# Gated linear attention on 64x64 tiles of the TensorE array, in steps by head pairs

## The chip, the cores and the metric

The kernel runs on one NeuronCore of a Trainium2 chip. The metric is device time in microseconds (us) of one execution. Lower is better.

## The reference, cut to what matters

The kernel is one whole layer: normalization, one large projection, three attention branches, a gated merge, an output projection, and a squared-ReLU MLP, on 512 frames of 1024 channels. The change is in branch A, gated linear attention, with 4 heads, 64 key channels, 128 value channels and chunks of 64 frames:

```python
b = jnp.cumsum(log_a, axis=2)              # inside each chunk of 64
e_pos, e_neg = jnp.exp(b), jnp.exp(-b)
q_pos = qc * e_pos
a_causal = einsum('bnthd,bnshd->bnhts', q_pos, kc * e_neg)
a_anti   = einsum('bnthd,bnshd->bnhts', qc * e_neg, kc * e_pos)
attn = jnp.where(lower, a_causal, a_anti)
o_intra = einsum('bnhts,bnshv->bnthv', attn, vc)
chunk_kv = einsum('bnshd,bnshv->bnhdv', kc * jnp.exp(b_last - b), vc)
state    = state * chunk_decay + chunk_kv   # scan over 8 chunks; prev is the state before each
o_inter  = einsum('bnthd,bnhdv->bnthv', q_pos, prev)
o = o_intra + o_inter                       # then RMSNorm by head and a SiLU gate
```

Per head and chunk the products are small: scores contract over 64 channels, states over 64 frames, and the read of a state (the chunk product) over 64 channels.

## The kernel before

TensorE's order is the program's order; the other engines are scheduled by the framework. The large products split each operand into a high and a low part and run three matmuls (`mm3`, L151 to L153). Weights stream in as chunks of 128x1024: a DMA, a cast to the high part on ScalarE (L142), a subtraction for the low part on VectorE (L143).

The attention of branch A stands in the block `with pool("gla")`. Its work is a list of 20 steps, which `weave` mixes with 96 units of filling: the gate and output projection of the memory branch (`branch("gate_mem", ...)`). A unit is one `mm3`. After step i (counted from 0) the filling is brought up to 96 × (i + 1) // 20 units, so that about five units lie behind each step. An `idle` step is filling alone.

Heads go in pairs: pair j holds heads 2j and 2j + 1, whose 64 channels share the 128 partitions of the projected q and k (`gqT[j]`, `gkT[j]`). The steps are:

- `decays(j)`: sums of log decays on TensorE (L686), three exponentials, and the scaled keys `kn`, `kp`, `kd`. The scaled queries `qpos[e]`, `qneg[e]` exist once per head e of the pair (L707, L708): the other head's 64 partitions are zero, filled once by GpSimd (L677, L678).
- `key_turn(j)`: four transposes of `kd` (L715), copied to two tiles, `kdE` for even chunks (VectorE, L716) and `kdO` for odd chunks (ScalarE, L717). Each is zero in the other half of its partitions (L679, L680).
- `gla_scores(h)`: four matmuls for the causal and four for the mirrored scores (L748). Each takes all 128 partitions, of which the zeros in `qpos[e]` leave one head. The masks select from both into the tile `at`, in copies of 128x128 (L750).
- `states(j)`: sixteen matmuls over all 128 partitions, 64 columns each; the two heads' results go to the two partition halves (L729). VectorE then runs the scan into `prev` (L734, L736).
- `gla_values(h)`: per block of two chunks the scores times v, full width (L759; the first block in two halves, L763), alternating with the two chunk products `qpos` times `prev` of 64 columns each (L765). Square, sum, reciprocal root (GpSimd, L231) and scaling to `on` (L774) follow.
- `gla_turn(h)`: four transposes of `on` (L780), the gate (L782) and a split for the output projection.

PSUM tiles of these steps come from `at_()`, four banks in rotation.

Of the kernel before, what the change touches and what calls it, by code (L numbers as in the profile page):

```python
# [9 lines left out]
F32 = mybir.dt.float32  # L10
# [3 lines left out]
AF = mybir.ActivationFunctionType  # L14
ALU = mybir.AluOpType
AX = mybir.AxisListType

P = 128
D = 1024
S = 512  # L20
M = 256
KT = D // P
NT = S // P
# [38 lines left out]
def hybrid_block(ctx, tc, chunks, wst, xT, memT, xN, cols, gffn, gfin, wup, cst, out):  # L62
    nc = tc.nc
# [5 lines left out]
    def nm(s):  # L69
        uid[0] += 1  # L70
        return f"{s}_{uid[0]}"
# [13 lines left out]
    def at_(shape=None):  # L85
        return pa.tile(shape or [P, 512], F32, tag="a", name=nm("a"))
# [140 lines left out]
    def rsqrt(pool_, ss, inv, n):  # L227
        ms = pool_.tile([P, n], F32, tag="ms", name=nm("ms"), bufs=2)
        r = pool_.tile([P, n], F32, tag="rr", name=nm("rr"), bufs=2)
        nc.vector.tensor_scalar(ms, ss, inv, EPS, op0=ALU.mult, op1=ALU.add)  # L230
        nc.gpsimd.tensor_tensor(r, ms, mhalf[:, :n], op=ALU.pow)  # L231
        return r
# [34 lines left out]
    with pool("front") as fp:  # L267
# [24 lines left out]
        ps = at_()  # L292
# [375 lines left out]

    with pool("gla") as lp:
        NC = 8  # L670
        qpos = [lp.tile([P, S], F32, name=f"qpos{e}") for e in range(2)]
        qneg = [lp.tile([P, S], F32, name=f"qneg{e}") for e in range(2)]
        kdE = lp.tile([P, NT, P], F32, name="kdE")
        kdO = lp.tile([P, NT, P], F32, name="kdO")
        for e in range(2):
            b = slice(64 - 64 * e, 128 - 64 * e)
            nc.gpsimd.memset(qpos[e][b], 0.0)  # L677
            nc.gpsimd.memset(qneg[e][b], 0.0)  # L678
        nc.gpsimd.memset(kdE[64:128], 0.0)  # L679
        nc.gpsimd.memset(kdO[0:64], 0.0)  # L680
        gs = {}

        def decays(j):
            pb = at_()
            for t in range(NT):
                nc.tensor.matmul(pb[:, t * P:(t + 1) * P], la[:, t, j * P:(j + 1) * P], tri64, start=True, stop=True)  # L686
            ep = lp.tile([P, S], F32, tag="ep", name=nm("ep"))
            en = lp.tile([P, S], F32, tag="en", name=nm("en"))
            bl = small(lp, NC, "bl").rearrange("p (c o) -> p c o", o=1)
            dec = small(lp, NC, "dec")  # L690
            ek = lp.tile([P, NC, 64], F32, tag="ek", name=nm("ek"))
            pb3 = pb.rearrange("p (c t) -> p c t", c=NC)
            nc.vector.tensor_copy(bl, pb3[:, :, 63:64])
            nc.vector.tensor_tensor(ek, pb3, bl.to_broadcast([P, NC, 64]), op=ALU.subtract)
            nc.scalar.activation(ep, pb, AF.Exp)
            nc.scalar.activation(en, pb, AF.Exp, scale=-1.0)
            nc.scalar.activation(ek, ek, AF.Exp, scale=-1.0)
            nc.scalar.activation(dec, bl.rearrange("p c o -> p (c o)"), AF.Exp)
            kn = lp.tile([P, S], F32, tag="kn", name=nm("kn"))
            kp = lp.tile([P, S], F32, tag="kp", name=nm("kp"))  # L700
            kd = lp.tile([P, S], F32, tag="kd", name=nm("kd"))
            nc.vector.tensor_tensor(kd, gkT[j], ek.rearrange("p c t -> p (c t)"), op=ALU.mult)
            nc.vector.tensor_tensor(kn, gkT[j], en, op=ALU.mult)
            nc.vector.tensor_tensor(kp, gkT[j], ep, op=ALU.mult)
            for e in range(2):
                a = slice(64 * e, 64 * e + 64)
                nc.vector.tensor_tensor(qpos[e][a], gqT[j][a], ep[a], op=ALU.mult)  # L707
                nc.vector.tensor_tensor(qneg[e][a], gqT[j][a], en[a], op=ALU.mult)  # L708
            gs["d", j] = dec, kn, kp, kd

        def key_turn(j):
            kd = gs["d", j][3]
            pk = at_([P, NT, P])
            for t in range(NT):
                nc.tensor.transpose(pk[:, t, :], kd[:, t * P:(t + 1) * P], ident)  # L715
            nc.vector.tensor_copy(kdE[0:64], pk[0:64])  # L716
            nc.scalar.copy(kdO[64:128], pk[64:128])  # L717

        def states(j):
            dec = gs["d", j][0]  # L720
            prev = gs["s", j] = lp.tile([P, NC, P], F32, tag="prev", name=nm("prev"))
            for g in range(2):
                pv = at_([P, 4, P])
                for i in range(4):
                    c = 4 * g + i
                    t = c // 2
                    for e in range(2):
                        h = 2 * j + e
                        nc.tensor.matmul(pv[64 * e:64 * e + 64, i, :], (kdO if c % 2 else kdE)[:, t, 64 * e:64 * e + 64],  # L729
                                         gv[:, t, h * P:(h + 1) * P], start=True, stop=True)  # L730
                for i in range(4):
                    c = 4 * g + i
                    if c == 0:
                        nc.vector.tensor_copy(prev[:, 1, :], pv[:, 0, :])  # L734
                    elif c < NC - 1:
                        nc.vector.scalar_tensor_tensor(prev[:, c + 1, :], prev[:, c, :], dec[:, c:c + 1], pv[:, i, :],  # L736
                                                       op0=ALU.mult, op1=ALU.add)

        def gla_scores(h):
            j, e = divmod(h, 2)  # L740
            _, kn, kp, _ = gs["d", j]
            pc, pn = at_([P, NT, P]), at_([P, NT, P])
            at = gs["a", h] = lp.tile([P, NT, P], F32, tag="at", name=nm("at"), bufs=2)
            nc.gpsimd.memset(at, 0.0)
            for m, (ps, kk, qq) in enumerate(((pc, kn, qpos[e]), (pn, kp, qneg[e]))):
                for t in range(NT):
                    sl = slice(t * P, (t + 1) * P)
                    nc.tensor.matmul(ps[:, t, :], kk[:, sl], qq[:, sl], start=True, stop=True)  # L748
                for t in range(NT):
                    nc.vector.copy_predicated(at[:, t, :], msk_s[:, m, :], ps[:, t, :])  # L750

        def gla_values(h):
            j, e = divmod(h, 2)
            at, prev = gs["a", h], gs["s", j]
            po = at_([P, NT, P])
            for t in range(NT):
                vt = gv[:, t, h * P:(h + 1) * P]
                if t:
                    nc.tensor.matmul(po[:, t, :], at[:, t, :], vt, start=True, stop=False)  # L759
                for c in (2 * t, 2 * t + 1):  # L760
                    r = slice(64 * (c % 2), 64 * (c % 2) + 64)
                    if t == 0:
                        nc.tensor.matmul(po[r, t, :], at[:, t, r], vt, start=True, stop=c == 0)  # L763
                    if c:
                        nc.tensor.matmul(po[r, t, :], qpos[e][:, 64 * c:64 * c + 64], prev[:, c, :], start=False,  # L765
                                         stop=True)
            sq = lp.tile([P, NT, P], F32, tag="sq", name=nm("sq"))
            ss = lp.tile([P, NT], F32, tag="ss", name=nm("ss"), bufs=2)
            nc.scalar.activation(sq, po, AF.Square)
            nc.vector.tensor_reduce(ss, sq, axis=AX.X, op=ALU.add)  # L770
            r = rsqrt(lp, ss, 1.0 / P, NT)
            on = gs["o", h] = lp.tile([P, NT, P], F32, tag="on", name=nm("on"), bufs=2)
            for t in range(NT):
                nc.vector.tensor_scalar(on[:, t, :], po[:, t, :], r[:, t:t + 1], None, op0=ALU.mult)  # L774

        def gla_turn(h):
            on = gs["o", h]
            pt = at_()
            for t in range(NT):
                nc.tensor.transpose(pt[:, t * P:(t + 1) * P], on[:, t, :], ident)  # L780
            og = lp.tile([P, S], F32, tag="og", name=nm("og"))
            nc.vector.tensor_tensor(og, pt, sg[h], op=ALU.mult)  # L782
            split(ogh[h], ogl[h], og)

        def idle(_):
            pass

        steps = [partial(fn, i) for fn, i in (
            (decays, 0), (idle, 0), (idle, 0), (key_turn, 0), (gla_scores, 0), (states, 0), (gla_scores, 1), (gla_values, 0), (gla_values, 1),
            (decays, 1), (gla_turn, 0), (gla_turn, 1), (key_turn, 1), (gla_scores, 2), (states, 1), (gla_scores, 3),  # L790
            (gla_values, 2), (gla_values, 3), (gla_turn, 2), (gla_turn, 3))]
        weave(steps, 96, branch("gate_mem", "w_mem_o", omh, oml, 1))
    gst.close()
    omst.close()
# [452 lines left out]
```

## Time and profile before

| | |
|---|---|
| median of 3 runs | 866.18 us (865.49 to 867.07) |
| span of the profiled execution, first to last instruction | 862.5 us |
| what lies around the span (median less span) | 3.7 us |
| TensorE clock granted, mean | 0.990 |
| the 20 steps with their filling | about 318 to 409 us of the span |

The time of the profiled execution itself is known by its span alone; the median is from executions without the profiler. In the profile, PE is the matmuls of TensorE and PEld its weight loads, which overlap; DVE is VectorE, ACT ScalarE, POOL GpSimd, SP the queue that issues most DMAs. `L729` is line 729 of the kernel. `out<-in` names the tiles, `x32` counts instructions. `a` stands for the PSUM tiles of `at_()`, `mm` for those of the large products. In the chain of waits a row is the start, the length, and the piece of work on the path that ended last.

### The profile page before, as it was taken

How to read it: one execution, taken by the hardware profiler on the slowest of the kernel's cores; microseconds unless marked ns; L12 is line 12 of the kernel's file. 1: busy time of each engine (PE TensorE's matmuls, PEld its weight loads, DVE VectorE, ACT ScalarE, POOL GpSimd, SP SyncE). 2: the span in 40 equal slices, each digit the busy share in tenths (PEclk: the TensorE clock that was granted, in tenths of full speed). 3: DMA queues.
4: the chain of work that ended last, by engine and by line, in shares of the span. 5: the costliest groups of instructions: out<-in, count | busy, mean ns of one | idle time of the engine just before them, and what ended most of it. 6: DMA issues, size and time to landing. Idle time of an engine off the chain costs nothing.

```text
span 862.5 us, 11811 instructions
## 1 busy us (share of the span) xinstructions
PE 839.0 (97%) x4513; PEld 711.2 (82%) x4513; DVE 542.4 (63%) x850; ACT 440.3 (51%) x703; POOL 113.0 (13%) x130
## 2 busy tenths in 40 slices
PE   8999999999999999999999999999999999999993
PEld 6778788888888888787888889888997899799872
DVE  5784656756444546474533547675688678778954
ACT  7764746754333432321332436565676377457744
POOL 5100000000000021221112100111001000100234
PEclk9999999999999999999999999999999999999997
DMA  8444745544547355336222413758757956785694
GB/s 320 145 150 168 201 135 178 146 171 123 171 133 230 125 150 168 97 113 231 98 98 98 170 50 118 225 124 204 243 171 162 265 199 171 179 256 176 138 170 133
DMA packets 37513, 142.37 MB, mean 165 GB/s; under 512 B 4592, under 2 KB 5392, under 8 KB 35728
## 3 DMA queue, kind: packets, MB, share of 16 engines
q1 hardware_dynamic: 27216, 93.36, 30.5%
q0 software_dynamic: 8448, 45.09, 24.8%
q10 hardware_dynamic: 1792, 3.16, 1.1%
q8 instruction: 35, 0.57, 0.3%
q14 instruction: 22, 0.18, 0.1%
HBM read 136.34 MB, written 27.28 MB: 190 GB/s over the span
## 4 chain that ended last, share of the span: by engine, by line
PE 74%; issue 12%; DMA 6%; DVE 3%; ACT 2%; POOL 1%; SPq 0%; POOLq 0%; ACTq 0%; DVEq 0%
PE mm L152 20%; PE mm L153 20%; PE mm L151 20%; DMA b<-in_wst_dram 6%; PE a L151 2%; PE a L152 2%; PE a L153 2%; ACT hi L203 1%; PE a L748 1%; DVE lo L204 1%; PE a L477 1%; DMA cst_s<-in_cst_dram 1%; PE a L765 1%; PE a L508 1%; PE a L507 1%
## 5 line engine op out<-in xcount | busy, mean ns | idle before, releaser
L143 DVE TENSOR_TENSOR wlo<-raw,whi 128x1024 fp32r<-128x1024 f32 x80 | 101.7, 1275 | 104.1 <-ACT whi L142 103.5
L142 ACT CAST whi<-raw 128x1024 fp32r<-128x1024 f32 x80 | 84.1, 1053 | 132.3 <-PE mm L152 100.3
L151 PE MATMUL mm<-uhi,whi 128*128 128x512 f32 x360 | 142.5, 396 | 0.0
L152 PE MATMUL mm<-ulo,whi 128*128 128x512 f32 x360 | 140.7, 391 | 1.4 <-DVE ulo L204 1.4
L153 PE MATMUL mm<-uhi,wlo 128*128 128x512 f32 x360 | 140.5, 390 | 0.0
L203 ACT CAST hi<-raw 128x1024 fp32r<-128x1024 f32 x58 | 60.5, 1048 | 44.7 <-PE mm L152 31.7
L204 DVE TENSOR_TENSOR lo<-raw,hi 128x1024 fp32r<-128x1024 f32 x58 | 70.6, 1222 | 17.6 <-ACT hi L203 17.6
L152 PEld LDWEIGHTS mm<-ulo,whi 128*128 128x128 f32 x360 | 67.7, 188 | 15.8 <-DVE ulo L204 2.9
L153 PEld LDWEIGHTS mm<-uhi,wlo 128*128 128x128 f32 x360 | 67.6, 188 | 14.6 <-DVE wlo L143 0.4
L151 PEld LDWEIGHTS mm<-uhi,whi 128*128 128x128 f32 x360 | 67.7, 188 | 13.5 <-issue 0.7
L204 DVE TENSOR_TENSOR lo<-b,hi 128x1024 fp32r<-128x1024 f32 x40 | 48.9, 1223 | 38.3 <-ACT hi L203 38.2
L203 ACT CAST hi<-b 128x1024 fp32r<-128x1024 f32 x40 | 41.9, 1048 | 57.5 <-PE mm L153 24.1
L152 PE MATMUL mm<-lo,ch 128*128 128x512 f32 x160 | 63.4, 396 | 2.5 <-DVE lo L204 2.5
L151 PE MATMUL mm<-hi,ch 128*128 128x512 f32 x160 | 63.1, 395 | 0.9 <-ACT hi L203 0.8
L153 PE MATMUL mm<-hi,cl 128*128 128x512 f32 x160 | 63.0, 394 | 0.0
L1050 POOL DMA_DIRECT2D b<-in_wst_dram x32 | 27.7, 865 | 267.1 <-DVE lo L204 210.2
L152 PE MATMUL mm<-u2l,hi 128*128 128x256 f32 x192 | 54.3, 283 | 0.0
L153 PE MATMUL mm<-u2h,lo 128*128 128x256 f32 x192 | 54.3, 283 | 0.0
L151 PE MATMUL mm<-u2h,hi 128*128 128x256 f32 x192 | 54.3, 283 | 0.0
L151 PE MATMUL mm<-u2sh,hi 128*128 128x256 f32 x144 | 40.8, 283 | 0.0
L152 PE MATMUL mm<-u2sl,hi 128*128 128x256 f32 x144 | 40.8, 283 | 0.0
L153 PE MATMUL mm<-u2sh,lo 128*128 128x256 f32 x144 | 40.8, 283 | 0.0
(349 smaller groups left out, 1945.5 us busy)
## 6 DMA issues: line engine op xcount, KB each, us to landing
raw<-in_wst_dram SPq DMA_DIRECT2D x122, 512.0 KB, 4.0
b<-in_wst_dram POOLq DMA_DIRECT2D x32, 512.0 KB, 5.3
T<-in_wst_dram POOLq DMA_DIRECT2D x12, 1024.0 KB, 8.4
raw<-T SPq DMA_DIRECT2D x24, 512.0 KB, 4.5
b<-in_wst_dram SPq DMA_DIRECT2D x16, 512.0 KB, 5.1
xr<-in_xT_dram SPq DMA_DIRECT2D x4, 512.0 KB, 8.1
nFb<-dF ACTq DMA_DIRECT2D x8, 256.0 KB, 3.8
h<-in_xN_dram SPq DMA_DIRECT2D x4, 512.0 KB, 7.6
```

Source lines behind the costliest of these rows:

```text
L142: cast = nc.scalar.copy(hi, raw)
L143: nc.vector.tensor_tensor(lo, raw, f(hi), op=ALU.subtract)
L151: nc.tensor.matmul(ps, lh, rh, start=start, stop=False)
L152: nc.tensor.matmul(ps, lh, rl, start=False, stop=False)
L153: nc.tensor.matmul(ps, ll, rh, start=False, stop=stop)
L203: nc.scalar.copy(hi, src)
L204: return nc.vector.tensor_tensor(lo, src, f(hi), op=ALU.subtract).ins
L477: nc.tensor.matmul(ps[:, :w], q, K[e][:, 1, :w], start=False, stop=True)
L507: nc.tensor.matmul(po[:, q0:], vv, PTh[:, c0:c0 + w], start=n == 0, stop=False)
L508: nc.tensor.matmul(po[:, q0:], vv, PTl[:, c0:c0 + w], start=False, stop=n == 3)
L748: nc.tensor.matmul(ps[:, t, :], kk[:, sl], qq[:, sl], start=True, stop=True)
L1050: nc.gpsimd.dma_start(to, x, accum_op=ALU.add)
```

## The change

The zero padding goes. `qpos` and `qneg` are one tile for a pair, `kdT` replaces `kdE` and `kdO`, and the memsets for zeros are gone. Every small matmul names its 64 partitions (`half[e]`): scores contract over 64 rows, and the two heads of a pair stand next to each other in the order, writing to two banks. States and chunk products contract over 64 rows and write 64 columns, a quadrant of the array each, again to two banks. A score call now takes a pair and one of the two masks, and its masked copy covers four blocks at once. `gla_values` takes a pair: first all products of scores and v, then all chunk products, then both heads' normalization. The list still has 20 steps, with two `idle` in place of two steps.

```diff
-        qpos = [lp.tile([P, S], F32, name=f"qpos{e}") for e in range(2)]
-        qneg = [lp.tile([P, S], F32, name=f"qneg{e}") for e in range(2)]
-        kdE = lp.tile([P, NT, P], F32, name="kdE")
-        kdO = lp.tile([P, NT, P], F32, name="kdO")
...
+        qpos, qneg = (lp.tile([P, S], F32, name=n) for n in ("qpos", "qneg"))
+        kdT = lp.tile([P, NT, P], F32, name="kdT")
+        half = [slice(64 * e, 64 * e + 64) for e in range(2)]
...
-            for e in range(2):
-                a = slice(64 * e, 64 * e + 64)
-                nc.vector.tensor_tensor(qpos[e][a], gqT[j][a], ep[a], op=ALU.mult)
-                nc.vector.tensor_tensor(qneg[e][a], gqT[j][a], en[a], op=ALU.mult)
+            nc.vector.tensor_tensor(qpos, gqT[j], ep, op=ALU.mult)
+            nc.vector.tensor_tensor(qneg, gqT[j], en, op=ALU.mult)
...
-            nc.vector.tensor_copy(kdE[0:64], pk[0:64])
-            nc.scalar.copy(kdO[64:128], pk[64:128])
+            nc.scalar.copy(kdT, pk)
...
+            pv = [at_([P, 4, P]) for _ in range(2)]
+            for t in range(NT):
+                for o in range(2):
                     for e in range(2):
                         h = 2 * j + e
+                        nc.tensor.matmul(pv[o][half[e], t, :], kdT[half[o], t, half[e]], gv[half[o], t, h * P:(h + 1) * P],
+                                         start=True, stop=True)
...
+        def gla_scores(j, m):
             _, kn, kp, _ = gs["d", j]
+            kk, qq = ((kn, qpos), (kp, qneg))[m]
...
+            ps = [at_([P, NT, P]) for _ in range(2)]
+            for t in range(NT):
+                sl = slice(t * P, (t + 1) * P)
+                for e in range(2):
+                    nc.tensor.matmul(ps[e][:, t, :], kk[half[e], sl], qq[half[e], sl], start=True, stop=True)
+            for e in range(2):
+                nc.vector.copy_predicated(gs["a", j][e], msk_s[:, m:m + 1, :].to_broadcast([P, NT, P]), ps[e])
+
+        def gla_values(j):
+            ats, prev = gs["a", j], gs["s", j]
+            pos = [at_([P, NT, P]) for _ in range(2)]
+            for e in range(2):
+                h = 2 * j + e
                 for t in range(NT):
+                    nc.tensor.matmul(pos[e][:, t, :], ats[e][:, t, :], gv[:, t, h * P:(h + 1) * P], start=t == 0, stop=t == 0,
+                                     skip_group_check=True)
+            for c in range(1, NC):
+                for e in range(2):
+                    nc.tensor.matmul(pos[e][half[c % 2], c // 2, :], qpos[half[e], 64 * c:64 * c + 64], prev[half[e], c, :],
+                                     start=False, stop=True, skip_group_check=True)
...
+        steps = [partial(fn, *i) for fn, *i in (
+            (decays, 0), (idle, 0), (idle, 0), (key_turn, 0), (gla_scores, 0, 0), (states, 0), (gla_scores, 0, 1), (idle, 0),
+            (gla_values, 0), (decays, 1), (gla_turn, 0), (gla_turn, 1), (key_turn, 1), (gla_scores, 1, 0), (states, 1),
+            (gla_scores, 1, 1), (idle, 0), (gla_values, 1), (gla_turn, 2), (gla_turn, 3))]
```

More of the change, by code (lines that the diff above doesn't have):

```diff
@@ L670, in hybrid_block @@
         NC = 8
-        qpos = [lp.tile([P, S], F32, name=f"qpos{e}") for e in range(2)]
-        qneg = [lp.tile([P, S], F32, name=f"qneg{e}") for e in range(2)]
-        kdE = lp.tile([P, NT, P], F32, name="kdE")
-        kdO = lp.tile([P, NT, P], F32, name="kdO")
-        for e in range(2):
[L676 to L680, printed above, removed]
+        qpos, qneg = (lp.tile([P, S], F32, name=n) for n in ("qpos", "qneg"))
+        kdT = lp.tile([P, NT, P], F32, name="kdT")
+        half = [slice(64 * e, 64 * e + 64) for e in range(2)]
         gs = {}
@@ L704, in decays @@
             nc.vector.tensor_tensor(kp, gkT[j], ep, op=ALU.mult)
-            for e in range(2):
-                a = slice(64 * e, 64 * e + 64)
-                nc.vector.tensor_tensor(qpos[e][a], gqT[j][a], ep[a], op=ALU.mult)
-                nc.vector.tensor_tensor(qneg[e][a], gqT[j][a], en[a], op=ALU.mult)
+            nc.vector.tensor_tensor(qpos, gqT[j], ep, op=ALU.mult)
+            nc.vector.tensor_tensor(qneg, gqT[j], en, op=ALU.mult)
             gs["d", j] = dec, kn, kp, kd
@@ L721, in states @@
             prev = gs["s", j] = lp.tile([P, NC, P], F32, tag="prev", name=nm("prev"))
[L722 to L726, printed above, removed]
+            pv = [at_([P, 4, P]) for _ in range(2)]
+            for t in range(NT):
+                for o in range(2):
                     for e in range(2):
                         h = 2 * j + e
[L729 to L737, printed above, removed]
@@ L739, in gla_scores @@
-        def gla_scores(h):
-            j, e = divmod(h, 2)
-            _, kn, kp, _ = gs["d", j]
[L742 to L745, printed above, removed]
-                for t in range(NT):
-                    sl = slice(t * P, (t + 1) * P)
-                    nc.tensor.matmul(ps[:, t, :], kk[:, sl], qq[:, sl], start=True, stop=True)
-                for t in range(NT):
-                    nc.vector.copy_predicated(at[:, t, :], msk_s[:, m, :], ps[:, t, :])
@@ L752, in gla_values @@
[L752 to L774, printed above, removed]
@@ new lines, in states @@
+                        nc.tensor.matmul(pv[o][half[e], t, :], kdT[half[o], t, half[e]], gv[half[o], t, h * P:(h + 1) * P],
+                                         start=True, stop=True)
+            nc.vector.tensor_copy(prev[:, 1, :], pv[0][:, 0, :])
+            for c in range(1, NC - 1):
+                nc.vector.scalar_tensor_tensor(prev[:, c + 1, :], prev[:, c, :], dec[:, c:c + 1], pv[c % 2][:, c // 2, :],
+                                               op0=ALU.mult, op1=ALU.add)
+        def gla_scores(j, m):
+            _, kn, kp, _ = gs["d", j]
+            kk, qq = ((kn, qpos), (kp, qneg))[m]
+            if m == 0:
+                gs["a", j] = [lp.tile([P, NT, P], F32, tag="at", name=nm("at"), bufs=2) for _ in range(2)]
+                for at in gs["a", j]:
+                    nc.gpsimd.memset(at, 0.0)
+            ps = [at_([P, NT, P]) for _ in range(2)]
[5 more added lines that the diff above has]
+                nc.vector.copy_predicated(gs["a", j][e], msk_s[:, m:m + 1, :].to_broadcast([P, NT, P]), ps[e])
@@ new lines, in gla_values @@
+        def gla_values(j):
[3 more added lines that the diff above has]
+                h = 2 * j + e
+                for t in range(NT):
+                    nc.tensor.matmul(pos[e][:, t, :], ats[e][:, t, :], gv[:, t, h * P:(h + 1) * P], start=t == 0, stop=t == 0,
[4 more added lines that the diff above has]
+                                     start=False, stop=True, skip_group_check=True)
+            for e in range(2):
+                h, po = 2 * j + e, pos[e]
+                sq = lp.tile([P, NT, P], F32, tag="sq", name=nm("sq"))
+                ss = lp.tile([P, NT], F32, tag="ss", name=nm("ss"), bufs=2)
+                nc.scalar.activation(sq, po, AF.Square)
+                nc.vector.tensor_reduce(ss, sq, axis=AX.X, op=ALU.add)
+                r = rsqrt(lp, ss, 1.0 / P, NT)
+                on = gs["o", h] = lp.tile([P, NT, P], F32, tag="on", name=nm("on"), bufs=2)
+                for t in range(NT):
+                    nc.vector.tensor_scalar(on[:, t, :], po[:, t, :], r[:, t:t + 1], None, op0=ALU.mult)
@@ L786, in idle @@
             pass
[L788 to L791, printed above, removed]
+        steps = [partial(fn, *i) for fn, *i in (
+            (decays, 0), (idle, 0), (idle, 0), (key_turn, 0), (gla_scores, 0, 0), (states, 0), (gla_scores, 0, 1), (idle, 0),
+            (gla_values, 0), (decays, 1), (gla_turn, 0), (gla_turn, 1), (key_turn, 1), (gla_scores, 1, 0), (states, 1),
+            (gla_scores, 1, 1), (idle, 0), (gla_values, 1), (gla_turn, 2), (gla_turn, 3))]
         weave(steps, 96, branch("gate_mem", "w_mem_o", omh, oml, 1))
```

## The prediction

> **What bounds the kernel now.** I read the page's busy times first, then its groups, then the view of who waited for whom, then the chain of waits inside the stage that the change touches (about 318 to 409 us), and last single instructions there.
>
> ```profile
> span 862.5 us, 11811 instructions
> PE 839.0 (97%) x4513; PEld 711.2 (82%) x4513; DVE 542.4 (63%) x850; ACT 440.3 (51%) x703; POOL 113.0 (13%) x130
> L142 ACT CAST whi<-raw 128x1024 fp32r<-128x1024 f32 x80 | 84.1, 1053 | 132.3 <-PE mm L152 100.3
> ```
>
> TensorE is busy for 97% of the span. The scalar engine's casts of new weights spend 100.3 us waiting for TensorE to release a buffer: supply waits for TensorE, not the reverse. In the stage itself, ten-microsecond windows show how much room the others have (columns: engine, busy time, number of instructions):
>
> ```profile
> 340.00:350.00 10.00, 10.00 (x63) 7.89 (x63) 5.80 (x17) 1.54 (x2) 0.81 (x1) 1.00 0.35 118
> 380.00:390.00 10.00, 10.00 (x77) 8.46 (x76) 6.83 (x16) 2.70 (x3) 2.12 (x2) 1.00 0.36 68
> sum 110.00, PE 110.00 PEld 89.00 DVE 64.17 ACT 30.82 POOL 23.31; mean PE 10.00 PEld 8.09 DVE 5.83 ACT 2.80 POOL 2.12
> ```
>
> The order is TensorE, weight loads, VectorE, ScalarE, GpSimd, then granted clock (1.00) and DMA share. TensorE is busy for all 110 us of the eleven windows, VectorE for 64, DMA for about a third. So a microsecond taken from TensorE here is a microsecond of the run, as long as nothing becomes late. The chain of waits gives the start and length of each piece:
>
> ```profile
> 337.30 1.90 PE a L729 x32
> 339.20 0.43 PE mm L151
> 339.63 0.23 PE mm L152
> 342.14 1.78 PE a L748 x16
> 347.34 0.37 PE a L763 x4
> 347.71 0.22 PE a L765 x2
> 347.93 0.42 PE a L759 x2
> 348.35 0.37 PE a L765 x4
> ...
> 349.50 0.42 PE a L759 x2
> 349.92 0.37 PE a L765 x4
> 350.29 0.43 PE mm L151
> ```
>
> L748 is scores of one head, L729 the states of one pair, and the pieces from 347.34 to 350.29 the values of one head. An F32 matmul shows as two MATMUL instructions ("passes"): L729 issues 16 matmuls and has x32.
>
> Three prices follow. **A pass alone** is 0.11 us: L765 x2 takes 0.22, and L748 1.78/16 = 0.11. **A change of tile shape**: a round of L765 x4 and L759 x2 takes 0.37 + 0.42 = 0.79. Its two full passes are 0.22, its four half-width passes two at a time another 0.22, which leaves 0.35 for going into the small tiles and out. The states agree: 1.90, plus the 0.20 by which the L151 behind them exceeds an ordinary 0.23, less 16 × 0.11 = 1.76, leaves 0.34. **Passes side by side**: that the 32 passes of L729 fit into 1.90 us says that two 64-column tiles already work at once. Short windows over their start show it directly:
>
> ```profile
> 337.23 0.33 PE L729 MATMUL a<-gv,kdE 128*64 128x128 f32 x2
> 337.23 0.14 PEld L729 LDWEIGHTS a<-gv,kdE 128*64 128x64 f32 x2 [0.35 <-issue]
> L729 PEld LDWEIGHTS a<-gv,kdE x32: 132/137/137, 337.2 to 382.3; 128*64 128x64 f32 x32
> L748 PEld LDWEIGHTS a<-qpos,kn x32: 187/192/192, 331.7 to 387.0; 128*128 128x128 f32 x32
> ```
>
> Two products and two weight loads begin together. Though the code issues head 0 entirely before head 1, the second head's first pass doesn't wait for the first head's second one. Both loads are over in 0.14 us, the length of one.
>
> **The change part by part, on TensorE.** Before, from those pieces: four heads' scores, 4 × 1.78 = 7.12. Two pairs' states, 2 × (1.90 + 0.20) = 4.20. Four heads' values, 4 × (350.29 − 347.34 + 0.20) = 12.60. Together 23.9 us. Transposes and decay sums stay.
>
> After, *scores*: four calls of 8 matmuls, 16 passes each on two 64-row tiles. Row tiles occur nowhere in this trace. The bounds for a pass are 0.11 (one at a time, as L748) and 0.055 (two at once, as L729). I take 0.055, because the nearest row, the column tiles of L729, shares the array that way. Each call enters and leaves a shape, 0.35; before, scores ran in the shape of their neighbours and paid nothing. 4 × (16 × 0.055 + 0.35) = 4.92.
>
> *States*: the same 32 passes a pair, but in four quadrants, to two banks. Bounds for a pass: 0.11 (no overlap), 0.055 (two at once as now), 0.0275 (four). I take four: L729's pair started together against the order of the code, so each tile seems to run its own queue. 2 × (32 × 0.0275 + 0.35) = 2.46.
>
> *Values*: per pair 8 full matmuls, 16 passes × 0.11 = 1.76. Then 14 quadrant matmuls in one go; odd chunks fill one column half with four matmuls a head, 8 × 0.11 = 0.88. One change of shape and back, 0.35, where each head paid for four. 2 × (1.76 + 0.88 + 0.35) = 5.98.
>
> Sum after: 13.4. Gain on TensorE 23.9 − 13.4 = 10.5 us. The eight changes of shape are priced from column tiles. Into row tiles the price could be nothing (2.8 us more gain) or twice as much (2.8 less).
>
> **What becomes late.** The rows of the last head's values, where the reciprocal root and normalization follow the products:
>
> ```profile
> 400.62 0.60 ACT L769 ACTIVATE sq<-a 128x512 f32<-128x512 f32 x1 [2.28 <-PE a L765]
> 401.25 0.69 DVE L770 TENSOR_REDUCE ss<-sq 128x4 f32<-128x512 f32 x1 [2.14 <-ACT sq L769]
> 401.97 0.17 DVE L230 TENSOR_SCALAR ms<-ss 128x4 f32<-128x4 f32 x1
> 402.29 1.00 POOL L231 TENSOR_TENSOR rr<-ms,cst_s 128x4 f32<-128x4 f32 x1 [5.52 <-DVE ms L230]
> 403.48 1.12 DVE L774 TENSOR_SCALAR on<-a,rr 128x128 f32<-128x128 f32 x4
> 397.88 1.23 DVE L143 TENSOR_TENSOR wlo<-raw,whi 128x1024 fp32r<-128x1024 f32 x1
> ```
>
> From 400.62, when the products release the square, to 404.60 is 4.0 us; the first of four slices is there after 3.1. Before, ten units of filling (each three matmuls of 0.23, 0.69 us) lay between a head's values and its turn. Now the second pair's values sit one step ahead of the turn of head 2: step 18 of 20 is due at 86 units, step 17 at 81, so five units, 3.45 us. The second head's reduction (0.69 + 0.17) or a weight split (1.23) may come in between on VectorE. The wait is between nothing and 4.0 + 0.86 + 1.23 − 3.45 = 2.6 us; I take 0.8. Behind the waiting transposes stand that step's fill and, later, the last branch. The first pair has more than two steps and a decay sum in between; no wait there.
>
> **Other engines.** These rows give what goes:
>
> ```profile
> L750 DVE COPY_PREDICATED at<-msk_s,a x32: 289/295/305, 333.1 to 390.3; 128x128 f32<-128x128 uint8 x32
> L707 DVE TENSOR_TENSOR qpos<-gqT,ep x4: 676/682/690, 321.9 to 365.4; 64x512 f32<-64x512 f32 x4
> L716 DVE COPY kdE<-a x2: 677/680/683, 328.7 to 374.1; 64x512 f32<-64x512 f32 x2
> L717 ACT COPY kdO<-a x2: 580/582/583, 329.4 to 374.8; 64x512 f32<-64x512 f32 x2
> ```
>
> 32 masked copies become 8 of four times the width, each between 0.30 and 1.18 us (0.69 is what other 128x512 operations take here): 9.4 us become about 5.5. Eight half-height products become four full ones, 2.7 us less, since 64 partitions cost what 128 would. The kdE copy leaves VectorE, 0.68 a pair; ScalarE's copy covers all partitions at 0.58. The zero fills on GpSimd go. All of this lies under TensorE's 110 of 110, so it counts as nothing; if that cover were gone, it would be gain. Scores and states now take two PSUM banks together where four are in rotation; each has a step of 3 us or more for its copies. No DMA is added or moved. The 12 weight chunks of the stage come some 10 us faster at a DMA share of about 0.35, and the casts have waiting to give away.
>
> **Sum.** 10.5 − 0.8 = 9.7 us. The profiled execution spans 862.5, and the median of the runs is 866.2; the 3.7 between lies outside the first and last instruction and stays. 866.2 − 9.7 = **856.5 us** (span about 852.8).
>
> **The rivals.** *Two at a time.* Quadrants gain nothing over L729's rate: passes leave at 0.055. Scores 4.92, states 2 × (1.76 + 0.35) = 4.22, values 2 × (1.76 + 28 × 0.055 + 0.35) = 7.30, together 16.4; 7.5 − 0.8 = 6.7, **859.5**. For it: no row here shows more than two at once. Against it: the starts in pairs.
> The Trainium skill, "TensorE: Matmul & The Clock Gate", section "Back-to-back issue gap", says that the sequencer's program spends about 62 ns on each matmul when hardware decoding is off. By that rate the sum would be 5.4 us of gain, near this rival, but L729's 55 ns is under it.
>
> *Weight loads one at a time.* A 128-column load has 192 ns against 137 for 64 columns, so 64 columns stream in about 55 ns and 128 in 110. If tiles must load in turn, 128-column scores fall back to 0.11 a pass: 4 × (1.76 + 0.35) = 8.44. States and values are as in the last case; 20.0 in all. 3.9 − 0.8 = 3.1, **863.1**. Against it: L729's two loads over in 0.14 us, but those were column tiles.
> The same page of the Trainium skill, "LDWEIGHTS (loading the stationary operand)", holds that a load costs by its columns, not its rows; the trace's 192 and 137 agree on the columns, and no run here shows fewer rows.
>
> *Slower: 64-row passes don't overlap at all.* Each of the 64 + 64 + 56 = 184 passes of scores, states and chunk products takes the array alone, the zero padding's saving is nil and the column overlap of today is lost. Scores 8.44, states 2 × (3.52 + 0.35) = 7.74, values 2 × (1.76 + 3.08 + 0.35) = 10.38: 26.6, or 2.7 more than before; with the wait 3.5 slower, **869.7**. The price decides from the point where 23.9 − 0.8 − 8 × 0.35 − 3.52 = 16.8 us spread over 184 passes, 0.091 us a pass. The alone rate of 0.11 is above it, the paired 0.055 far below.
>
> *Same:* the gain comes but a late operand or a different order on VectorE eats it later. For it: weight splits do stop TensorE here and there. Against: the waits below are small and far from this stage. **866**.
>
> ```profile
> PEld mm L152 <- DVE lo L204: 4.4, 5, 1.1
> PEld mm L153 <- DVE wlo L143: 0.4, 1, 0.4
> ```
>
> **Chances.** Forecast 0.62, two at a time 0.16, loads in turn 0.12, slower 0.06, same 0.04. Faster by over 0.2% (1.7 us, about what a measurement can tell from no change) 0.90, within 0.04, slower 0.06. Forecast and second case hold only 0.78, so the range reaches to the third, 863.3. Downwards it takes no wait (0.8) and half of the 2.8 for shapes: 854.3.
>
> **What would show it.** Scores in pieces of x16 at about 0.9 to 1.2 us, four of them. States x32 under 1.2 us with four products starting together. No alternation of full and half tiles inside values. A TensorE wait for `on` ahead of the third turn, under 2.6 us. Wrong would be: states still at 1.9 (two at a time), scores at 1.8 or more (loads in turn), states at 3.5 (none at once), or TensorE idle in the stage behind.

## The result and the profile after

| | before | changed kernel |
|---|---|---|
| median time, us (4 runs each) | 865.84 (863.99 to 867.07) | 856.38 (854.98 to 858.21) |
| ratio, 95% interval | | 0.9896 [0.9872, 0.9921] |
| span of the profiled execution, us | 862.5 | 853.5 |
| the stage, us | 90.8 | 81.3 |

The change makes the kernel faster by 1.0% (0.8 to 1.3%). "The stage" is used from here on: from the start of the first decay sum to the end of the last transposition, both read from the chain of waits. Its ends before:

```profile
317.78 0.89 PE a L686 x8
...
408.10 0.44 PE a L780 x4
```

That is 408.54 − 317.78 = 90.76 us. In the changed kernel, the chain of waits over the stage, without the filling between its steps:

```profile
318.89 0.89 PE a L679 x8
...
333.21 1.09 PE a L735 x16
334.30 0.43 PE mm L151
337.93 1.03 PE a L717 x32
338.96 0.43 PE mm L151
...
350.07 1.78 PE a L745 x16
...
351.85 1.02 PE a L749 x28
352.87 0.43 PE mm L151
...
395.16 0.11 issue
395.26 1.01 PE a L766 x4
399.72 0.44 PE a L766 x4
```

L735 is a score call of a pair, L717 the states of a pair, L745 the full products and L749 the chunk products of a pair. The pieces of 1.78, 1.02 and 0.43 follow each other without the changes between full and half tiles that the old values had. The stage is 399.72 + 0.44 − 318.89 = 81.27 us, 9.49 less. The first transposition of the last pair, 1.01 instead of 0.44 and with 0.11 ahead, is the wait for the normalization.

The span went down by 9.0, not 9.49. The stage starts 1.11 us later than before (318.89 against 317.78), and what follows it took 853.45 − 400.16 = 453.3 us, against 453.9. Single profiles can't put either down to the change: in the ten profiles of this study the stage starts between 317.8 and 322.0 us, with the same TensorE work ahead of it, and what follows it takes 452.1 to 456.5 us. The two kernels with the old tiles have the longest ends (453.9 and 456.5; the other eight up to 453.4), so a small part of that may belong to the change. No run settles it.

The other engines, by the page's first line and the windows at the same places as in the prediction:

```profile
PE 827.1 (97%) x4505; PEld 702.7 (82%) x4505; DVE 536.0 (63%) x820; ACT 439.8 (52%) x703; POOL 111.2 (13%) x124
```

```profile
380.00:390.00 10.00, 10.00 (x63) 8.32 (x62) 5.50 (x8) 2.59 (x3) 2.92 (x2) 1.00 0.82 211
340.00:350.00 10.00, 10.00 (x56) 8.06 (x55) 6.64 (x12) 1.55 (x2) 1.32 (x3) 1.00 0.49 131
```

In these windows TensorE is still busy without a gap, at a granted clock of 1.00; over the whole stage it is idle for 0.12 us, at the turn of the last pair. Its busy time fell by 11.9 us, more than the span. With windows cut at the ends of the stage, 9.6 of that lie in the stage, 0.5 ahead of it and 1.7 behind it; outside the stage the number of its instructions is the same, and why they were busy for less is not shown. In all, its instructions fell by eight only: the first block of a head's values, four passes in two halves before, now takes two passes, and the other products are the same in number, packed.

### The profile page after: what moved, and what is told of

Same layout as the page of the kernel before. It is cut to its first block, busy times and chain, and to the rows that moved or that the text cites. A ratio compares the mean times of both kernels' runs of the same rounds, so it can differ in the third digit from the quotient of the medians.

```text
span 853.5 us, 11749 instructions
## 1 busy us (share of the span) xinstructions
PE 827.1 (97%) x4505; PEld 702.7 (82%) x4505; DVE 536.0 (63%) x820; ACT 439.8 (52%) x703; POOL 111.2 (13%) x124
## 4 chain that ended last, share of the span: by engine, by line
PE 70%; issue 12%; DMA 8%; DVE 4%; ACT 3%; POOL 1%; SPq 0%; POOLq 0%; ACTq 0%; DVEq 0%
PE mm L152 20%; PE mm L151 19%; PE mm L153 19%; DMA b<-in_wst_dram 7%; PE a L152 2%; PE a L151 2%; PE a L153 2%; DVE lo L204 1%; ACT hi L203 1%; DMA h<-s 1%; POOL h L1036 1%; PE a L477 1%; DMA memr<-in_memT_dram 1%; PE a L508 1%; PE a L507 1%
## 5 line engine op out<-in xcount | busy, mean ns | idle before, releaser
L151 PE MATMUL mm<-uhi,whi 128*128 128x512 f32 x360 | 142.6, 396 | 0.0
L151 PEld LDWEIGHTS mm<-uhi,whi 128*128 128x128 f32 x360 | 67.7, 188 | 13.8 <-issue 0.5
L151 PE MATMUL mm<-hi,ch 128*128 128x512 f32 x160 | 62.4, 390 | 0.0
L151 PE MATMUL mm<-u2h,hi 128*128 128x256 f32 x192 | 54.3, 283 | 0.0
L151 PE MATMUL mm<-u2sh,hi 128*128 128x256 f32 x144 | 40.8, 283 | 0.0
```

What stands on the lines that cost most here:

```text
L151: nc.tensor.matmul(ps, lh, rh, start=start, stop=False)
```

## The experiments

Each edit is to the changed kernel unless it says otherwise. All stages at a glance:

| kernel | scores, a call | states, a pair | stage, us | time, us (before beside it) |
|---|---|---|---|---|
| before | 1.78 (one head, both masks) | 1.90 | 90.76 | 865.84 |
| changed | 1.09 (a pair, one mask) | 1.03 | 81.27 | 856.38 (865.84) |
| scores on 128 rows | 1.78 | 1.03 | 83.17 | 856.79 (864.28), one run |
| before, values grouped | 1.78 | 1.90 | 86.63 | 864.71 (864.28), one run |
| tile by tile | 1.64 | 2.50 | 86.38 | 863.62 (864.28), one run |
| states on 128 rows | 1.09 | 1.90 | 82.92 | 857.34 (864.28), one run |
| in twos | 1.19 | 1.10 | 81.79 | 855.05 (864.76), one run |
| values earlier | 1.09 | 1.03 | 80.61 | 854.68 (865.09) |
| scores joined | 1.99 (two calls) | 1.03 | 80.44 | 854.04 (865.09) |
| joined and earlier | 1.99 (two calls) | 1.03 | 79.75 | 852.72 (865.09) |

The stage settles what single times can't. Six runs of one kernel ("values earlier") lie between 851.67 and 859.99, while pieces of the stage repeat within 0.02 us from profile to profile.

### Scores back on 128 rows

```diff
-                    nc.tensor.matmul(ps[e][:, t, :], kk[half[e], sl], qq[half[e], sl], start=True, stop=True)
+                    nc.tensor.matmul(ps[e][:, t, :], kk[:, sl], qq[e][:, sl], start=True, stop=True)
```

with `qpos` and `qneg` once per head and zeros in the other head's half.

> The changed kernel with its scores put back on all 128 rows, over queries padded with zeros; states and values stay on 64-row tiles. Measure: the stage, from the start of the first decay sum to the end of the last transposition in the chain of waits (81.3 us in the changed kernel, 90.8 before). Theory (two row tiles share the array, and each call pays a change of shape): a score call goes from 1.09 + 0.20 behind it to 1.78 and nothing behind it, four calls, so the stage is 2.0 us longer, 83.2. Rival (the scores gave nothing, all of the gain is in the values): 81.3, with scores at 1.3 a call or less either way.

Chain of waits; the two score calls of the first pair, with the states between them:

```profile
333.93 1.78 PE a L740 x16
335.71 0.23 PE mm L151
...
339.12 1.03 PE a L722 x32
...
343.14 1.78 PE a L740 x16
```

A call takes 1.78, and the L151 behind it its ordinary 0.23. The stage is 402.78 − 319.61 = 83.17, 1.90 longer than with row tiles. The theory's 83.2 holds: row tiles are worth 1.9 of the 9.5 us.

### States back on 128 rows

```diff
-                        nc.tensor.matmul(pv[o][half[e], t, :], kdT[half[o], t, half[e]], gv[half[o], t, h * P:(h + 1) * P],
+                        nc.tensor.matmul(pv[o][half[e], t, :], (kdO if o else kdE)[:, t, half[e]], gv[:, t, h * P:(h + 1) * P],
```

> The changed kernel with its states put back on 128 rows over two zero-padded copies of the turned keys, two column tiles at once. Theory (four quadrants halve what two column tiles took): states 1.03 back to 1.90 a pair, stage 1.7 us longer, 83.0. Rival (the quadrants are bound elsewhere, the gain is from the change of order): stage within 0.5 us of 81.3.

```profile
338.24 1.90 PE a L721 x32
```

The states take what they took before. The stage is 402.12 − 319.20 = 82.92, 1.65 longer. Quadrants against two column tiles are worth 1.65 us.

### The kernel before, with its values grouped

```diff
             for t in range(NT):
-                vt = gv[:, t, h * P:(h + 1) * P]
-                if t:
-                    nc.tensor.matmul(po[:, t, :], at[:, t, :], vt, start=True, stop=False)
-                for c in (2 * t, 2 * t + 1):
...
+                nc.tensor.matmul(po[:, t, :], at[:, t, :], gv[:, t, h * P:(h + 1) * P], start=t == 0, stop=t == 0,
+                                 skip_group_check=True)
+            for c in range(1, NC):
+                r = slice(64 * (c % 2), 64 * (c % 2) + 64)
+                nc.tensor.matmul(po[r, c // 2, :], qpos[e][:, 64 * c:64 * c + 64], prev[:, c, :], start=False, stop=True,
+                                 skip_group_check=True)
```

> The kernel before, with one thing changed: each head's values do the four full products first and then all seven chunk products, which keep their zero padding and 128 rows. Theory (most of the values' old cost was going in and out of the small tiles): a head's values fall from 3.15 to 8 x 0.11 + 8 x 0.11 + 0.35 = 2.1 us, the stage from 90.8 to 86.6, some 4.2 of the 6.6 us that the values gained. Rival (the quadrants gave the gain, the order nothing): stage above 90.

One head's values in its chain of waits:

```profile
349.33 0.89 PE a L757 x8
350.22 1.02 PE a L761 x14
351.24 0.43 PE mm L151
```

0.89 + 1.02 + 0.20 = 2.11 where 3.15 were, four times; the stage is 406.40 − 319.77 = 86.63. So 4.1 us of the gain need no new tile at all, only an order that goes into the small tiles once. The rest of the values' gain, 4 × 2.11 − 2 × 3.00 = 2.4 us, comes with the pair and its quadrants; this is a difference, and no run takes the two apart. This kernel's one time, 864.71, is no faster than the 864.28 beside it, though its stage is 4.1 us shorter: its stage started 2.0 us later than in the profile of before, and 456.5 us followed it, against 453.9. What made the rest longer is not shown. A single time doesn't carry such a question.

### Tile by tile

```diff
-            for t in range(NT):
-                for o in range(2):
-                    for e in range(2):
+            for o in range(2):
+                for e in range(2):
+                    for t in range(NT):
```

and the same for the scores: all of one head, then all of the other.

> The changed kernel, with the same matmuls in another order: states one quadrant after the other (four matmuls in a row on the same tile), scores one head after the other. Chunk products keep their order. Theory (each tile has a queue of its own and TensorE looks far ahead in its order): states stay at 1.03 us a pair, scores at 1.09 a call, stage 81.3. Rival (it looks ahead by a few instructions only, and what is next to each other in the order runs side by side): states 2.5 to 3.5 a pair, scores up to 1.8 a call, stage 85 to 89.

```profile
336.36 1.64 PE a L735 x16
...
341.64 2.50 PE a L717 x32
```

The theory fell. The same 32 passes on the same four quadrants take 2.50 us instead of 1.03, and the stage is 408.42 − 322.04 = 86.38: 5.1 us, more than half of the gain, lost by the order of lines alone. Short windows at the start of the states show why. In the changed kernel, 0.05 us after the start:

```profile
337.86 0.34 PE L717 MATMUL a<-gv,kdT 64*64 64x128 f32 x4
```

and tile by tile, 0.05 and then 0.43 us after the start:

```profile
341.57 0.32 PE L717 MATMUL a<-gv,kdT 64*64 64x128 f32 x1
...
341.57 0.65 PE L717 MATMUL a<-gv,kdT 64*64 64x128 f32 x4
```

Four products begin at once in the one; in the other one begins, and four have begun only after 0.43 us, one behind another. In the trace the starts of single passes lie at 0, 0.160, 0.269, 0.378, 0.487 and 0.493 us: five passes of the first quadrant, and 6 ns after the fifth the first of the next. At that moment three passes of the first quadrant's eight had not started. The next two quadrants repeat it: the fifth pass of one at 0.981 and 1.474 us, the first of the next at 0.986 and 1.480. I read this as a limit: TensorE does run ahead of a waiting pass, and so departs from the order of the program, but not past a fourth one on the same tile.

### In twos

```diff
-            for t in range(NT):
-                for o in range(2):
-                    for e in range(2):
+            for t2 in range(0, NT, 2):
+                for o in range(2):
+                    for e in range(2):
+                        for t in (t2, t2 + 1):
```

and the same for the scores.

> The changed kernel with the states and scores issued in twos: two matmuls (four passes) in a row on a tile, then the next tile. In the run that went tile by tile, a tile's first pass started with the fifth pass of the tile ahead, so that three passes of that tile were waiting. Theory (each tile holds three passes that wait, and the order of the program is stopped only by a fourth): four passes in a row fit one tile, so all tiles work at once, states 1.03 us a pair, scores 1.09 a call, stage 81.3. Rival (about three passes are looked ahead in all, whatever their tile): about two tiles at once, states 1.7 to 1.9 a pair, stage some 1.5 us longer, 82.8; scores near 1.1 by both.

```profile
332.98 1.19 PE a L737 x16
...
337.81 1.10 PE a L718 x32
```

Four passes in a row on a tile cost 0.07 us a pair in the states and 0.10 a call in the scores; the stage is 400.45 − 318.66 = 81.79. Were three passes the limit over all tiles, the states would have stood near 1.8. So the limit is kept for each tile. The small excess, 4 × 0.10 + 2 × 0.07 = 0.54 us, was expected by neither side, but the trace of the states shows where it arises. The first quadrant's fifth pass starts at 0.488 us, as in the changed kernel (0.487). The weight loads for the fifth passes of the other three start only at 0.493 to 0.519 us, where they started at 0.388 to 0.402, and the sixth passes there come 0.05 to 0.06 us late. That fits the same limit: the second round puts passes five to eight on the first quadrant, the eighth finds a place only when the fifth has started, and the other quadrants stand behind it in the order. No further run tests this.

### Values earlier, scores joined, and both

```diff
-            (gla_scores, 1, 1), (idle, 0), (gla_values, 1), (gla_turn, 2), (gla_turn, 3))]
+            (gla_scores, 1, 1), (gla_values, 1), (idle, 0), (gla_turn, 2), (gla_turn, 3))]
```

> The changed kernel with one step moved: the second pair's values run one step earlier, so that ten units of filling lie ahead of head 2's turn and five between the last masked copies and the values. Theory (the turn waited 0.6 us for the normalization, and the masked copies have time to spare): no wait at that turn, no new one, stage 80.7. Rival (the products now wait for the masked copies on VectorE): a wait at the first full product of the second pair, stage 81.3 or longer. The time itself can't tell 0.6 us apart.

The turns of the last pair, in the chain of waits:

```profile
394.77 0.44 PE a L766 x4
398.67 0.44 PE a L766 x4
```

Both take 0.44 and nothing is ahead of them. No wait for masked copies turned up; the stage is 399.11 − 318.50 = 80.61, 0.66 shorter, as the theory had it. Time 854.68 us, 0.9885 of before [0.9858, 0.9913].

```diff
+        def both_scores(j):
+            gla_scores(j, 0)
+            gla_scores(j, 1)
...
-            (gla_scores, 0, 0), (states, 0), (gla_scores, 0, 1), (idle, 0),
+            (both_scores, 0), (states, 0), (idle, 0), (idle, 0),
```

and the same for the second pair.

> The changed kernel with both masks' score calls of a pair joined in one step: 32 passes on row tiles in one go. Theory (a call costs 16 x 0.055 and about 0.4 for going in and out): one going in and out less for each pair, the stage 0.8 us shorter, 80.5. Rival (the price of a call is in its passes, or four score banks at once make the states wait for masked copies): stage 81.3 or longer, in the second case with a wait ahead of the states.

```profile
333.54 1.99 PE a L735 x32
335.53 0.43 PE mm L151
```

Two calls in one take 1.99 + 0.20 = 2.19 instead of 2 × 1.29 = 2.58: 0.39 us is the price of going into row tiles and out once. The stage is 399.66 − 319.22 = 80.44, and no wait stands ahead of the states. Time 854.04 us, 0.9892 [0.9866, 0.9917].

> Both edits, joined scores and the second pair's values a step earlier. Theory: the two gains add, stage 79.9, time some 1.4 us under the changed kernel. Rival (one of them turns into a wait): stage 80.5 or more.

The stage is 398.35 − 318.60 = 79.75: 0.83 and 0.66 add to the 1.52 that was measured, within 0.03. Time 852.72 us (851.49 to 857.10), 0.9868 of before [0.9845, 0.9891]. It has the lowest median here, and the trace shows it ahead of the changed kernel by 1.5 us; the intervals of the two ratios overlap, so the times alone don't.

## Why the prediction was right, point by point

**The bound.** TensorE filled the stage before and after, so what left it left the span. That held: the stage lost 9.49 of the 9.7 us forecast, and what lies behind it did not get longer. The median, 856.38 against 856.5, is closer than the working deserves, and that is luck: the span was forecast at 852.8 and came at 853.5, and the 3.7 us around the span were too many. The profiled execution took 855.22 us with a span of 853.5, so 1.7 lie around it, and by the same 1.7 the profile of before was of an execution of about 864.2 us, some 2 us under the median used (an estimate).

**Pass prices.** States were forecast at 32 × 0.0275 + 0.35 = 1.23 us a pair and took 1.03 + 0.20 = 1.23. Values were forecast at 2.99 a pair and took 1.78 + 1.02 + 0.20 = 3.00. Scores were forecast at 1.23 a call and took 1.09 + 0.20 = 1.29. This is the term that was mis-sized: 0.04 of the 0.06 is the change of shape, since going into row tiles of 128 columns and out costs 0.39 (scores joined) and not the 0.35 of column tiles. Together 13.6 us against 13.4.

**The reason for four at once.** I argued that each tile seems to run its own queue, because L729's two heads started together against the order of the code. The number was right and the reason half of it: there is a place for each tile, but it holds three waiting passes, and the order of the program decides whether that is enough. Tile by tile, the same argument would have forecast 1.03 and missed by 1.5 us a pair. The changed kernel's order, neighbouring tiles next to each other with two passes each, is inside the limit. The rows that I had could not tell the two apart. Nor did the code of L729 issue one head entirely before the other, as the prediction says: it alternates the heads by single matmuls, so the row showed one waiting pass overtaken, and no more.
The Trainium skill, "TensorE: Matmul & The Clock Gate", section "The mechanism" under the packing of small matmuls, says that matmuls start and end strictly in program order. For the starts, this case's traces decide against it: tile by tile, the second quadrant's first pass starts at 0.493 us, ahead of three passes of the first quadrant that stand before it in the code. The ends in the profile are modelled and decide nothing.

**The wait.** Between nothing and 2.6 us, taken as 0.8: it is 0.66 by the kernel without it. The mechanism was the one named, the second pair's normalization one step ahead of its turn. What came in between on VectorE was not a weight split but the second head's reduction and L598, an operation of the filling:

```profile
393.58 0.69 DVE L756 TENSOR_REDUCE ss<-sq 128x4 f32<-128x512 f32 x1 [0.52 <-ACT sq L755]
394.18 0.68 DVE L598 SCALAR_TENSOR_TENSOR th<-th,mm 128x512 f32<-128x512 f32 x1
394.77 1.12 DVE L760 TENSOR_SCALAR on<-a,rr 128x128 f32<-128x128 f32 x4
```

The reciprocal root was ready at 394.23 us, and the scaling to `on` (L760) started behind L598. The 0.8 was a choice inside the range, and that it came so close is luck.

**What was to cost nothing.** It did. The masked copies are off the path, and their width was sized about right: 0.73 us, where 0.69 was taken.

```profile
L737 DVE COPY_PREDICATED at<-msk_s,a x8: 723/730/743, 334.4 to 383.9; 128x512 f32<-128x512 uint8 x8
```

The prediction misread one share: DMA was busy for about half of the old stage (0.51), not a third as in the two windows shown there. In the new stage it is 0.59, and TensorE waits there for no weight chunk.

**The rivals.** Two at a time would have left the states at 1.9 us, and 32 passes took 1.03, 32 ns each; so the slower rate for each matmul that the prediction set beside this rival did not bound this stretch either. Weight loads in turn would have left a score call at 1.8; it took 1.09, and the first two 128-column loads of a call start 7 ns apart and take 0.18 us each. The loads of all four quadrants, too, begin and end together:

```profile
337.86 0.15 PEld L717 LDWEIGHTS a<-gv,kdT 64*64 64x64 f32 x4 [0.35 <-issue]
```

Four loads within 0.15 us, one taking 0.13. The slower case, 0.11 us a pass without overlap, is out by a factor of four for the states. That the gain is lost behind the stage didn't happen.

**Where the gain came from.** By undoing single parts: row tiles for the scores 1.9 us, quadrants for the states 1.65, one visit to the small tiles in the values 4.1 (measured on the kernel before), the pair and its quadrants in the values 2.4 by difference, less the wait of 0.66. The sum is 9.4 of 9.49. The largest part is an order that the old tiles could have had too.

## What to carry to other kernels

Count the changes of tile shape before counting products: a visit to small tiles cost 0.35 to 0.39 us here, as much as three or four full passes of 128x128, so collect all work of one shape in one go. Put matmuls for different tiles next to each other in the order: four passes in a row on one tile cost 0.07 us a pair in the states, eight cost 1.47, because the tiles then ran largely one after another. Judge such edits by a stage in the trace whose pieces repeat within 0.02 us, when whole runs scatter by several microseconds.

## What the runs showed of the hardware

- Four 64x64 quadrants at once run four F32 passes of 128 columns in 0.109 us, the time of one, with the row halves writing to two banks: the starts on one tile lie 0.109 us apart, and 32 passes take 1.03 us. The four weight loads side by side take 0.15 us, one alone 0.13.
- As the starts of single passes read, a tile takes three waiting passes beside the running one, and a fourth stops the order of the program for all tiles (inferred from the tile-by-tile run, and borne out by the run in twos). Tile by tile, states went from 1.03 to 2.50 us and scores from 1.09 to 1.64.
- Going into small tiles and out costs about 0.35 us for column tiles and quadrants (states: 1.23 − 8 × 0.109 = 0.36) and 0.39 for row tiles, on top of the passes.
- The start of the stage moved between 317.8 and 322.0 us over ten profiles, with the same code ahead of it; that alone is 0.5% of the run.
